# Mixers in plain units, output pairs that open with both first products, and sums between products

## The chip, the cores and the metric

The program runs on one core of one Trainium2 chip. The metric is the device time of one execution in microseconds (us). The engines are named as in the profile: PE does the matmuls, PEld their weight loads, DVE is the vector engine, ACT the scalar engine, POOL the general one, and SP issues the DMAs that bring the weights.

## The reference

Two blocks stand one behind the other on 512 positions of width 1024; all data are fp32. The first is a hybrid mixer (gated delta rule and retention) with a network behind it. The second has two layers, each a network, a mixer and a network, with a layer norm behind each of the three; this is its core:

```python
def swiglu_2(x, w1, w2):
    g, u = jnp.split(x @ w1, 2, axis=-1)
    return (jax.nn.silu(g) * u) @ w2
def hybrid_mixer_2(...):
    b_gate, c_gate, v, x_r, y_r, g_logits = jnp.split(x @ w_in, SPLITS, axis=-1)
    y_a = (b_gate * causal_depthwise_conv(c_gate * v, sc_w, 3)) @ w_out_conv
    xc = causal_depthwise_conv(x_r, rc_w, 4) + rc_b
    gates = jax.nn.sigmoid(per_head(xc, rg_w) + rg_b)      # 4 heads of 256, two gates each
    log_a = -8.0 * gates[1] * jax.nn.softplus(-a_param)
    a = jnp.exp(log_a); mult = jnp.sqrt(-jnp.expm1(2.0 * log_a))
    h = linear_recurrence(a, xc * gates[0] * mult)         # h_t = a_t h_(t-1) + b_t
    y_b = (h * jax.nn.gelu(y_r)) @ w_out_rnn
    g_a, g_b = jnp.split(jax.nn.sigmoid(g_logits + b_merge), 2, axis=-1)
    return (g_a * y_a + g_b * y_b) @ w_o
```

So the program has five networks (swiglu, inner width 2816) and, in its second block, two of these mixers.

## The kernel before

**Products.** Every fp32 product is made of three matmuls on rounded halves: an operand x is split into hi (a cast on ACT) and lo = x − hi (a subtraction on DVE), and hi·hi, hi·lo and lo·hi are added up in PSUM. The weights arrive in fp32 by DMA, 512 KB at a time (a raw tile `wraw`), and are split on the chip into `whi`, `wlo` (some tiles of the same kind lie in the big tile `xa` that also holds the activations, and carry its name).

**A plain unit** is one block of 128 output columns: one weight (`load_w`: load, cast L43, subtraction L44) and `mm3` (L70 to L72), 24 matmuls of 128x512. Plain units are ordered by the automatic scheduler.

**A seven-quad** (class `Quad`) makes 2 by 2 output blocks at once (two groups of 128 columns each way, halves of 256 positions), with seven products in place of eight, as Strassen's method does. A product is 24 matmuls of 128x256 (`prod`, L134; 18 where the inner part has three blocks, 12 with two). Before it, sums of weights are made on DVE (`sum`, L164), each is cast on ACT (`cast`, L167) and its rest taken on DVE (`rest`, L169), and the activations need sums too (`Left.sums`, L120 to L126, split at L80 and L81). Behind a product, `after` moves it out of or between the PSUM banks (ACT, L180 to L184) and then runs the steps that use it.

**run_quads** writes the order of a list of quads by hand: PE, ACT, DVE and SP run in the order in which the program was written. Its position s is one product; with the product at s it emits the copies behind product s−1, then the due sums, the cast for product s+2, the due steps, and the rest for s+2. The four weight blocks of a quad are loaded together, six positions ahead.

**A network** (`ffn`): two quads' worth of columns run in plain units (`PLAIN=2`; silu and `h`, L285 and L289), the others in seven-quads. The inner width is done in the groups (0,3), (3,3), (6,2), (8,3) of (first quad, how many). Behind each of the first three groups come two output quads, the *output pair*: they multiply this group's `h` (its halves are `hl`) with the second weight. The first of a pair waits for the group's `h` (`needs`). The activation sums that the seven-quads want (`e.sums`, and `H.sum4` for the columns of the plain units) are made while the plain units run.

**A mixer** (`mixer`): two of the four heads of the recurrent branch are projected in plain units, then come 12 seven-quads (`run(0,2)`, `run(2,5)`, `run(5,12)`) for the rest of the input weight, with the recurrent gates (`rgates`: two sigmoids per tile L542 and L543, exp L547, tanh L548, sqrt L551, the recurrence, and a split into `uh`, `ul`) and the plain products with `w_or` and `w_oc` between them. The residual `X` is parked in DRAM during the mixer, as its tile holds the mixer's sum `z`.

The sequence of the trace in us: first block to about 1003 (its network from 671), network 1003 to 1382, mixer 1382 to 1963 (its seven-quads with what lies between them 1433 to 1865), networks to 2293 and to 2675, mixer 2675 to 3260 (seven-quads 2726 to 3161), last network to 3607.

Of the kernel before, what the change touches and what calls it, by code (L numbers as in the profile page):

```python
# [434 lines left out]
def mixer(e, w, w_rg, w_oc, w_or, w_o, C, ln):  # L435

    nc=e.nc
    with ExitStack() as cm:
        mx=cm.enter_context(e.tc.tile_pool(name="mx",bufs=1,reuse_waits="tile"))
        uh=mx.tile([P,8,512],F32R,name="uh"); ul=mx.tile([P,8,512],F32R,name="ul"); U=Flat(uh,ul)  # L440
        xg=lambda nm: mx.tile([P,2,516],F32,tag="xg",name=nm,bufs=7)

        z=e.X
        for m in range(8): nc.gpsimd.dma_start(e.xs[:,m,:],e.X[:,m,:])
        R={}
        def rec(hd):

            u=Use(); R[hd]=u
            def c11(ps):
                u.xp=xg("xp"); nc.gpsimd.memset(u.xp[:,:,0:3],0.0)  # L450
                nc.scalar.copy(u.xp[:,:,3:259],pair(ps))
            def c12(ps,E):
                t=tmp(e); nc.vector.tensor_add(t,ps,E)
                u.gy=xg("gy"); nc.scalar.activation(u.gy[:,:,0:256],pair(t),AF.Gelu_apprx_tanh)
            def c22(ps,E):
                t=tmp(e); nc.vector.tensor_sub(t,E,ps)
                u.t=t
            def c21(ps):
# [944 lines left out]
```

## Time and profile before

| | us |
|---|---|
| median of 3 runs (3608.77 to 3612.39) | 3608.95 |
| profiled execution | 3608.84 |
| its span in the trace | 3607.0 |
| PE busy in it | 3296.6 |
| DVE busy | 2788.0 |
| ACT busy | 1830.2 |

The profiled execution took 1.84 us more than its span, the time that lies around it, and is 0.11 us below the median. A busy share is a mean over stages with different limits; the stage that an edit touches has to be read by itself.

### The profile page before, as it was taken

The numbers are of one execution on the slowest core, as the hardware profiler recorded it, in microseconds if no ns is written. First come the engines' busy times: TensorE is split into PE (matmuls) and PEld (weight loads), VectorE is DVE, ScalarE is ACT, GpSimd is POOL, SyncE is SP. The second block draws the span as 40 slices with busy tenths as digits, with TensorE's granted clock in tenths as the row PEclk, the third lists the DMA queues.
The fourth block names the chain that finished last, engine by engine and source line by source line (L and its number), as shares of the span: only waits on it lengthen the run. The fifth ranks groups of instructions, "written<-read, shape, count | busy, mean of one in ns | idle before, by whom it ended". The sixth has DMA issues, their size and how long they took to land.

```text
span 3607.0 us, 58745 instructions
## 1 busy us (share of the span) xinstructions
PE 3296.6 (91%) x23808; PEld 3094.0 (86%) x23808; DVE 2788.0 (77%) x4333; ACT 1830.2 (51%) x2794; POOL 193.6 (5%) x237
## 2 busy tenths in 40 slices
PE   7889889899989999789899999989998798998998
PEld 3768779799989999688889999989997698898998
DVE  5957878799768888856767888788888657667887
ACT  5544435455445555853434455445557733444554
POOL 3231210000000000000000000000000000000000
PEclk9989999999999999999999999999999999999999
DMA  5221225133322242122241323223331232422322
GB/s 200 71 65 45 77 65 173 32 101 99 111 72 93 86 138 82 59 97 74 88 153 48 101 85 117 81 82 99 97 120 51 73 96 86 139 86 66 103 94 65
DMA packets 106080, 330.74 MB, mean 92 GB/s; under 512 B 11984, under 2 KB 15696, under 8 KB 105808
## 3 DMA queue, kind: packets, MB, share of 16 engines
q1 hardware_dynamic: 102464, 316.04, 27.1%
q0 software_dynamic: 3200, 10.49, 0.8%
q8 instruction: 187, 3.06, 0.4%
q14 instruction: 85, 0.70, 0.1%
q10 hardware_dynamic: 144, 0.45, 0.0%
HBM read 320.64 MB, written 6.29 MB: 91 GB/s over the span
## 4 chain that ended last, share of the span: by engine, by line
PE 64%; DVE 19%; ACT 8%; issue 4%; DMA 3%; POOL 1%; ACTq 0%; SPq 0%; DVEq 0%; POOLq 0%
PE sd L134 19%; PE pj L134 15%; PE pj L70 5%; PE pj L71 5%; PE pj L72 5%; DVE wlo L169 3%; PE sd L70 3%; PE sd L72 3%; PE sd L71 3%; DVE wraw L164 3%; DVE xa L169 2%; ACT whi L167 2%; ACT xa L167 1%; DVE cv L933 1%; DVE hl L81 1%
## 5 line engine op out<-in xcount | busy, mean ns | idle before, releaser
L169 DVE TENSOR_TENSOR wlo<-wraw,whi 128x1024 fp32r<-128x1024 f32 (+2 forms) x398 | 444.8, 1118 | 113.1 <-ACT whi L167 111.5
L134 PE MATMUL sd<-xa,whi 128*128 128x256 f32 x3136 | 428.6, 290 | 50.2 <-ACT sd L182 29.3
L167 ACT CAST whi<-wraw 128x1024 fp32r<-128x1024 f32 (+2 forms) x398 | 380.7, 963 | 147.4 <-DVE wraw L164 64.4
L134 PEld LDWEIGHTS sd<-xa,whi 128*128 128x128 f32 x3136 | 404.0, 197 | 58.4 <-ACT sd L182 31.7
L134 PE MATMUL pj<-xa,whi 128*128 128x256 f32 x2096 | 294.2, 296 | 54.6 <-ACT sd L180 40.3
L134 PEld LDWEIGHTS pj<-xa,whi 128*128 128x128 f32 x2096 | 278.7, 204 | 61.5 <-ACT sd L180 44.0
L134 PE MATMUL pj<-xa 128*128 128x256 f32 x1824 | 241.0, 290 | 30.8 <-ACT xa L167 11.9
L169 DVE TENSOR_TENSOR xa<-wraw,xa 128x1024 fp32r<-128x1024 f32 (+2 forms) x196 | 216.8, 1106 | 61.1 <-ACT xa L167 53.6
L70 PE MATMUL pj<-xa 128*128 128x256 f32 (+1 forms) x760 | 258.7, 343 | 3.1 <-ACT xa L80 1.7
L134 PEld LDWEIGHTS pj<-xa 128*128 128x128 f32 x1824 | 231.7, 198 | 34.7 <-ACT xa L167 13.7
L72 PE MATMUL pj<-xa 128*128 128x256 f32 (+1 forms) x760 | 258.6, 341 | 0.2 <-DVE xa L44 0.2
L71 PE MATMUL pj<-xa 128*128 128x256 f32 (+1 forms) x760 | 257.4, 339 | 0.1
L134 PE MATMUL sd<-xa 128*128 128x256 f32 x1920 | 247.1, 285 | 9.8 <-ACT sd L182 7.9
L134 PEld LDWEIGHTS sd<-xa 128*128 128x128 f32 x1920 | 239.2, 194 | 10.6 <-ACT sd L182 8.3
L167 ACT CAST xa<-wraw 128x1024 fp32r<-128x1024 f32 (+2 forms) x196 | 186.8, 953 | 99.7 <-DVE wraw L164 45.6
L134 PE MATMUL sd<-xa,wlo 128*128 128x256 f32 x1568 | 225.7, 288 | 0.0
L164 DVE TENSOR_TENSOR wraw<-wraw 128x1024 f32<-128x1024 f32 (+2 forms) x198 | 221.6, 1119 | 0.0
L134 PEld LDWEIGHTS sd<-xa,wlo 128*128 128x128 f32 x1568 | 208.0, 197 | 0.1
L43 ACT CAST xa<-wraw 128x1024 fp32r<-128x1024 f32 (+1 forms) x126 | 127.5, 1013 | 158.2 <-PE pj L71 101.5
L70 PEld LDWEIGHTS pj<-xa 128*128 128x128 f32 x760 | 147.3, 195 | 15.5 <-ACT xa L80 1.9
L71 PEld LDWEIGHTS pj<-xa 128*128 128x128 f32 x760 | 147.7, 194 | 10.6 <-DVE xa L81 0.5
L44 DVE TENSOR_TENSOR xa<-wraw,xa 128x1024 fp32r<-128x1024 f32 (+1 forms) x116 | 137.8, 1189 | 23.9 <-ACT xa L43 23.1
(570 smaller groups left out, 7699.1 us busy)
## 6 DMA issues: line engine op xcount, KB each, us to landing
wraw<-in_f_dram SPq DMA_DIRECT2D x176, 512.0 KB, 3.6
wraw<-in_f_dram SPq DMA_DIRECT2D x96, 384.0 KB, 3.1
wraw<-in_ff_dram SPq DMA_DIRECT2D x44, 512.0 KB, 3.7
wraw<-in_win_dram SPq DMA_DIRECT2D x32, 512.0 KB, 3.6
wraw<-in_w_xy_dram SPq DMA_DIRECT2D x32, 512.0 KB, 3.5
wraw<-in_w_cv_dram SPq DMA_DIRECT2D x32, 512.0 KB, 3.5
raw<-in_ada_dram SPq DMA_DIRECT2D x48, 256.0 KB, 2.8
wraw<-in_ff_dram SPq DMA_DIRECT2D x24, 384.0 KB, 3.2
```

The source lines that it names most:

```text
L43: nc.scalar.copy(hi[:,:n],raw[:,:n])
L44: (nc.gpsimd if e.wi%e.gp==0 else nc.vector).tensor_sub(lo[:,:n],raw[:,:n],hi[:,:n].bitcast(F32))
L70: nc.tensor.matmul(o,lhsT=hi[:,c],rhs=ah,start=start and k==k0,stop=False)
L71: nc.tensor.matmul(o,lhsT=hi[:,c],rhs=al,start=False,stop=False)
L72: nc.tensor.matmul(o,lhsT=lo[:,c],rhs=ah,start=False,stop=stop and k==nk-1)
L81: e.nc.vector.tensor_sub(lo,src,hi.bitcast(F32))
L134: nc.tensor.matmul(ps[:,p*256:p*256+256],lhsT=w[:,j:j+128],rhs=A.t[:,c,k,l,:],start=first,stop=last,skip_group_check=True)
L164: n=s.n; e.nc.vector.tensor_add(o[:,:n],x[:,:n],y[:,:n])
L167: s.w[j]=hilo_tile(e); e.nc.scalar.copy(s.w[j][0][:,:s.n],s.raw(j)[:,:s.n])
L169: hi,lo=s.w[j]; n=s.n; e.nc.vector.tensor_sub(lo[:,:n],s.raw(j)[:,:n],hi[:,:n].bitcast(F32))
L933: nc.vector.scalar_tensor_tensor(a[:,o0:o0+n],ci[:,o0+i:o0+i+n],sc(i),a[:,o0:o0+n],op0=ALU.mult,op1=ALU.add)
```

## The change

Both mixers of the second block lose their seven-quads: all their products are plain units, in a new function `mixer_in`. Heads are projected one ahead of their gates (`rproj(hd)`, then `rgates(hd-1)`), the gate projections and the products with `w_or` alternate, then the conv branch runs column by column. `z` has a tile of its own, so the parking of `X` falls away (32 DMAs on POOL's queue), and one of the recurrence's multiplications moves from DVE to POOL. The activation sums are no longer made in the mixers. The ring of raw weight tiles has four in the mixers instead of five, and in the networks seven as before.

In run_quads an output pair starts with product 1 of both its quads, behind the seventh product of the group's last quad as before; the second quad's first product is copied out while the first quad's seventh runs. A quad's loads come in three parts, its fifth sum's tile is taken when the sum is made, and cast and rest for position s+2 both stand behind the steps. Of the activation sums of a network, the second part and those of `h` of the plain units go between products (`extra`, positions 0 to 2 and 4 and 5); the first block's network keeps the former in the plain part.

```diff
-    def load(s,e):
+    def load(s,e,t):
         n=s.n; q=s.q
-        s.r12=load_raw(e,q[2],n); s.r22=load_raw(e,q[3],n); s.t3=e.wps[0][0].tile([P,1024],F32,tag="t3",name="t3",bufs=1); s.r11=load_raw(e,q[0],n); s.r21=load_raw(e,q[1],n)
+        if t==0: s.r11=load_raw(e,q[0],n)
+        if t==5: s.r12=load_raw(e,q[2],n); s.r22=load_raw(e,q[3],n);
+        if t==6: s.r21=load_raw(e,q[1],n)
     def sum(s,e,t):
+        if t==3: s.t3=e.fp.tile([P,1024],F32,tag="t3",name="t3",bufs=1)
         o,x,y={1:(s.r12,s.r12,s.r11),2:(s.r11,s.r11,s.t3),3:(s.t3,s.r12,s.r22),4:(s.r21,s.r21,s.r11)}[t]
         n=s.n; e.nc.vector.tensor_add(o[:,:n],x[:,:n],y[:,:n])
-    def raw(s,j): return (None,s.r11,s.r21,s.r11,s.r12,s.t3,s.r22,s.r21)[j]
+    def raw(s,j): return getattr(s,(None,"r11","r21","r11","r12","t3","r22","r21")[j])
...
-def run_quads(e, quads):
+def run_quads(e, quads, extra):
     ET=mybir.EngineType
-    seq=[]; left=None
-    for q in quads:
+    seq=[]; left=None; done=set()
+    for i,q in enumerate(quads):
         if q.needs and left: seq.append((left,7)); left=None
-        seq.append((q,1))
+        if q not in done: seq.append((q,1))
+        if q.needs: seq.append((quads[i+1],1)); done.add(quads[i+1])
         if left: seq.append((left,7))
         seq+=[(q,j) for j in (2,3,4,5,6)]; left=q
     seq.append((left,7))
     pos={(id(q),j):s for s,(q,j) in enumerate(seq)}
-    at={}
+    at={}; free=-99
     for q in quads:
-        a=pos[id(q),1]
-        for s,t in ((a-6,0),(a-3,3),(a-1,1),(a,2),(pos[id(q),5],4)): at.setdefault(s,[]).append((q,t))
+        g=lambda j: pos[id(q),j]
+        for s,t in ((g(1)-6,0),(g(3)-9,5),(g(2)-8,6),(max(g(3)-6,free),3),(g(3)-4,1),(g(3)-3,2),(g(5),4)): at.setdefault(s,[]).append((q,t))
+        free=g(5)-1
     with e.tc.manual_schedule(engines={ET.PE,ET.Activation,ET.DVE,ET.SP}):
-        for s in range(-6,len(seq)+1):
+        for s in range(min(at),len(seq)+1):
             for q,t in at.get(s,[]):
-                if t==0: q.load(e)
+                if t in (0,5,6): q.load(e,t)
+            put=None; keep=None
+            if s>0: put=seq[s-1]
             if 0<=s<len(seq):
                 q,j=seq[s]
                 for d in q.needs:
                     if j==1: d.all(6)
                     if j==3: d.all(7)
-                early=s>0 and j==2 and seq[s-1]==(q,1)
-                if early: q.after(e,1)
+                if j==2 and put==(q,1): q.after(e,1); put=None
                 q.mm(e,j)
-            else: early=False
-            if s>0 and not early: seq[s-1][0].after(e,seq[s-1][1])
+                if j==7 and s+1<len(seq) and seq[s+1][1]==2: keep=seq[s+1][0]
+            if put and not (put[1]==1 and put[0] in done): put[0].after(e,put[1])
             for q,t in at.get(s,[]):
-                if t: q.sum(e,t)
-            nx=seq[s+2] if 0<=s+2<len(seq) else None
-            if nx: nx[0].cast(e,nx[1])
+                if t in (1,2,3,4): q.sum(e,t)
             for q in quads:
                 for j in (2,5,6,7):
-                    if s>0 and (q,j)!=seq[s-1]: q.step(j)
-            if nx: nx[0].rest(e,nx[1])
+                    if s>0 and (q,j)!=put: q.step(j)
+            if keep in done: keep.after(e,1)
+            for f in extra.get(s,[]): f()
+            nx=seq[s+2] if 0<=s+2<len(seq) else None
+            if nx: nx[0].cast(e,nx[1]); nx[0].rest(e,nx[1])
...
+def htile(e): return e.fp.tile([P,4,256],F32,tag="h",name="h",bufs=3)
...
-                if j%2: into_left(e,H,j//2,hs[j//2],0 if sl is H0 else 1,True)
-        e.sums(0)
+                if j%2: into_left(e,H,j//2,hs[j//2],0 if sl is H0 else 1,False)
+        for i in range(4): e.sums(0,i)
         for j in range(halves,2*PLAIN):
             unit(j,FULL)
-            for half in (0,1): into_left(e,H,j//2,hs[j//2],half,True)
-        e.sums(1)
+            for half in (0,1): into_left(e,H,j//2,hs[j//2],half,False)
+        if e.early:
+            for i in range(4): e.sums(1,i)
...
-                run_quads(e,Q)
+                x={} if e.early else {0:[lambda: e.sums(1,0)],1:[lambda: e.sums(1,1)],2:[lambda: e.sums(1,2),lambda: e.sums(1,3)]}
+                for i,q in enumerate(range(PLAIN)): x[4+i]=[lambda q=q: H.sums(e,q,hs[q][:,0:2,:],hs[q][:,2:4,:])]
+                run_quads(e,Q,x)
...
-        run=lambda a,b: run_quads(e,[Quad(e.XA,q,4,u) for q,u in Q[a:b]])
...
-        rec(0).plain(w["xy"][0],(H0,H1))
-        e.sums(0)
-        rec(1).plain(w["xy"][1],(FULL,)); e.sums(1)
-        seven_mode(e); rgates(0); rgates(1)
-        run(0,2); rgates(2); rgates(3); run(2,5)
-        for m in range(8): orproj(m)
-        run(5,12)
...
+def mixer_in(e, mx, w_in, w_rg, w_oc, w_or, w_o, C, ln):
+    nc=e.nc; plain_mode(e,0)
+    uh=mx.tile([P,8,512],F32R,name="uh"); ul=mx.tile([P,8,512],F32R,name="ul"); U=Flat(uh,ul)
+    B_,C_,V_,XR,YR,GA,GB=[8*i for i in range(7)]
+    n=512
+    xp={}; gy={}; xc={}
+    def rproj(hd):
...
+            ps=psum(e); mm3(e,ps,W[key],0,KD,e.XA,sl)
...
+                nc.scalar.copy(xp[t][:,3+sl.start:3+sl.stop],ps[:,:m])
+            else:
+                if t not in gy: gy[t]=mx.tile([P,512],F32,tag="gy",name="gy",bufs=3)
+                nc.scalar.activation(gy[t][:,sl],ps[:,:m],AF.Gelu_apprx_tanh)
...
+        wg=load_w(e,w_rg[hd])
+        xc2=Flat(uh[:,2*hd:2*hd+2,:],ul[:,2*hd:2*hd+2,:])
+        gp={}
+        for i,t in enumerate((2*hd,2*hd+1)):
+            pr=psum(e,"ps"); mm3(e,pr,wg,512+i*128,2,xc2,FULL,stride=256)
+            pi=psum(e,"ps"); mm3(e,pi,wg,i*128,2,xc2,FULL,stride=256)
+            gr=tmp(e); nc.scalar.activation(gr,pr,AF.Sigmoid,bias=C["rg_b"][:,8+t:9+t])
+            gi=tmp(e); nc.scalar.activation(gi,pi,AF.Sigmoid,bias=C["rg_b"][:,t:t+1])
+            gp[t]=(gr,gi)
...
+        for t in (2*hd,2*hd+1):
+            gr,gi=gp[t]
+            a=tmp(e); nc.scalar.activation(a,gr,AF.Exp,scale=C["nsp"][:,t:t+1])
+            th=gr; nc.scalar.activation(th,gr,AF.Tanh,scale=C["psp"][:,t:t+1])
+            a2=tmp(e); nc.gpsimd.tensor_mul(a2,a,a)
+            nc.vector.scalar_tensor_tensor(th,a2,1.0,th,op0=ALU.add,op1=ALU.mult)
...
+            nc.gpsimd.tensor_mul(gi,gi,xc[t])
...
+    rproj(0)
+    for hd in range(1,4): rproj(hd); rgates(hd-1)
+    gbproj(0); rgates(3)
+    for m in range(1,3): gbproj(m)
+    for m in range(8):
+        if 3<=m+2<8 and m>0: gbproj(m+2)
+        orproj(m)
...
+        wc=load_w(e,w_in[C_+m]); pc=psum(e); mm3(e,pc,wc,0,KD,e.XA,FULL)
+        ct=tmp(e); nc.scalar.copy(ct,pc)
...
+        wb=load_w(e,w_in[B_+m]); pb=psum(e); mm3(e,pb,wb,0,KD,e.XA,FULL)
+        nc.vector.tensor_mul(u,u,pb)
...
+    A=e.gab
+    for m in range(A-1): gproj(m)
+    for m in range(8):
+        if m+A-1<8: gproj(m+A-1)
+        cproj(m)
...
-        e.gp=1<<30; wp2=pool("wp2"); e.wps=[(wp2,2)]; e.rps.append((wp2,1)); e.more=2
+        e.gp=1<<30; wp2=pool("wp2"); e.wps=[(wp2,2)]; e.more=3; e.gab=GAB
```

Counted over the whole program, PE has 4032 matmuls of 128x256 fewer (24 quads of 168) and 2304 of 128x512 more (96 units of 24); DVE has 184 additions and subtractions of 128x1024 fewer, ACT 88 casts of that size and 120 smaller operations.

**PE, first output pair of the second network** (the stretch around 1073 to 1097 us of the trace). `hl` is the split h; `pj` and `sd` are PSUM banks. Before:

```order
L134 MATMUL sd0_5192<-xa_85 128x256 x24
L134 MATMUL pj_10581<-hl_9851,whi_10533 128x256 x12
L134 MATMUL pj_10581<-hl_9851,wlo_10534 128x256 x6
L134 MATMUL pj_10581<-hl_9851,whi_10566 128x256 x12
L134 MATMUL pj_10581<-hl_9851,wlo_10567 128x256 x6
L134 MATMUL sd1_5193<-hl_9851,xa_85 128x256 x18
L134 MATMUL pj_10661<-hl_9851,whi_10625 128x256 x12
L134 MATMUL pj_10661<-hl_9851,wlo_10626 128x256 x6
```

After:

```order
L134 MATMUL sd0_5189<-xa_85 128x256 x24
L134 MATMUL pj_10577<-hl_9848,whi_10532 128x256 x12
L134 MATMUL pj_10577<-hl_9848,wlo_10533 128x256 x6
L134 MATMUL pj_10602<-hl_9848,whi_10565 128x256 x12
L134 MATMUL pj_10602<-hl_9848,wlo_10566 128x256 x6
L134 MATMUL pj_10577<-hl_9848,xa_85 128x256 x18
L134 MATMUL sd1_5190<-hl_9848,whi_10629 128x256 x12
L134 MATMUL sd1_5190<-hl_9848,wlo_10630 128x256 x6
```

Before, the second product of the first output quad went into the bank of its first (`pj_10581` twice); now the second quad's first product, in a bank of its own (`pj_10602`), stands between them.

**ACT, the first recurrent gates of the second block's first mixer** (around 1508 us of the trace). `t` are gates, `vec`, `nsp` and `psp` constants. Before:

```order
L542 ACT_TABLE_LOAD
L542 ACTIVATE t<-ps,vec_9810 128x512
L543 ACTIVATE t<-ps,vec_9810 128x512
L542 ACTIVATE t<-ps,vec_9810 128x512
L167 CAST whi<-wraw 128x1024
L543 ACTIVATE t<-ps,vec_9810 128x512
L547 ACT_TABLE_LOAD
L547 ACTIVATE t<-t,nsp_9812 128x512
L548 ACTIVATE t<-t,psp_9813 128x512
L80 CAST uh<-xc 128x1024
L551 ACT_TABLE_LOAD
L551 ACTIVATE t<-t 128x512
```

After, a little into the same work:

```order
L482 ACT_TABLE_LOAD
L482 ACTIVATE gy<-sd_5189 128x512
L497 ACT_TABLE_LOAD
L497 ACTIVATE t<-ps,vec_9807 128x512
L498 ACTIVATE t<-ps,vec_9807 128x512
L43 CAST xa<-wraw 128x1024
L502 ACT_TABLE_LOAD
L502 ACTIVATE t<-t,nsp_9809 128x512
L503 ACTIVATE t<-t,psp_9810 128x512
L479 COPY xp<-sd_5191 128x512
L506 ACT_TABLE_LOAD
L506 ACTIVATE t<-t 128x512
```

The gelu of the next head's projection (L482) now stands between the gates of this one, with a table load of its own; from the first gate to the last split of the branch there are 27 table loads, 49 activations of 128x512, 17 casts of 128x1024, 13 casts and 4 copies of 128x512 on ACT, beside 402 matmuls of 128x512 on PE.

**DVE, behind the plain part of the second network** (from 1050 us of the trace). `h` of the last plain unit, its split, then the sums. Before:

```order
L289 SCALAR_TENSOR_TENSOR h<-t,sd_5193 128x2x256
L164 TENSOR_TENSOR wraw<-wraw 128x1024
L81 TENSOR_TENSOR hl<-h,hl 128x2x256
L81 TENSOR_TENSOR hl<-h,hl 128x256
L120 TENSOR_TENSOR s<-h 128x256
L169 TENSOR_TENSOR wlo<-wraw,whi 128x1024
L121 TENSOR_TENSOR s<-s,h 128x256
L164 TENSOR_TENSOR wraw<-wraw,t_10337 128x1024
L123 TENSOR_TENSOR s<-s,h 128x256
L169 TENSOR_TENSOR wlo<-wraw,whi 128x1024
L81 TENSOR_TENSOR hl<-s,hl 128x4x256
```

After:

```order
L298 SCALAR_TENSOR_TENSOR h<-t,sd_5190 128x2x256
L167 TENSOR_TENSOR wraw<-wraw,t_10300 128x1024
L81 TENSOR_TENSOR hl<-h,hl 128x2x256
L81 TENSOR_TENSOR hl<-h,hl 128x256
L172 TENSOR_TENSOR wlo<-wraw,whi 128x1024
L122 TENSOR_TENSOR s<-X 128x256
L125 TENSOR_TENSOR s<-X 128x256
L126 TENSOR_TENSOR s<-s 128x256
L81 TENSOR_TENSOR xa<-s,xa 128x2x256
L172 TENSOR_TENSOR wlo<-wraw,whi 128x1024
```

The sums of the input (L122 to L126) now stand between the rests of the first quad's weights (L172), and the sums of `h` come later; from this `h` to the last split of the first quad's `h` DVE has 10 operations of 128x1024, 4 of 128x768, 10 of 128x512 and 21 of 128x256.

## Rows read from the trace of the kernel before

**Rows 1.** The page: span, and busy time of each engine with its instructions.

```profile
span 3607.0 us, 58745 instructions
PE 3296.6 (91%) x23808; PEld 3094.0 (86%) x23808; DVE 2788.0 (77%) x4333; ACT 1830.2 (51%) x2794; POOL 193.6 (5%) x237
```

**Rows 2.** Busy time by stage; columns are in the first row.

```profile
core 0: us, PE busy (x) PEld busy (x) DVE busy (x) ACT busy (x) POOL busy (x), PEclk, DMA share, GB/s
1003.00:1382.00 379.00, 360.07 (x2823) 352.21 (x2822) 308.20 (x411) 192.40 (x279) 0.00 (x0) 0.97 0.29 95
1433.00:1537.00 104.00, 75.63 (x464) 66.28 (x463) 83.17 (x101) 82.95 (x103) 9.10 (x14) 0.93 0.17 56
1433.00:1865.00 432.00, 375.26 (x2505) 347.66 (x2504) 300.33 (x330) 228.00 (x293) 15.39 (x28) 0.96 0.28 92
2293.00:2675.00 382.00, 362.50 (x2837) 354.25 (x2836) 314.94 (x426) 195.56 (x286) 0.00 (x0) 0.97 0.29 92
2726.00:3161.00 435.00, 378.20 (x2503) 350.51 (x2503) 300.24 (x329) 227.83 (x292) 15.45 (x28) 0.95 0.28 91
```

**Rows 3.** The same view of three short stretches, for the pace of matmuls.

```profile
1610.00:1650.00 40.00, 40.00 (x178) 33.14 (x177) 16.71 (x17) 7.38 (x7) 0.10 (x1) 1.00 0.25 81
1125.00:1175.00 50.00, 50.00 (x419) 50.00 (x418) 42.32 (x48) 27.79 (x37) 0.00 (x0) 1.00 0.27 85
1686.90:1690.30 3.40, 3.40 (x18) 3.40 (x17) 3.37 (x4) 0.84 (x2) 0.00 (x0) 0.50 0.02 5
```

**Rows 4.** PE's waits from 1433 to 1865: waited for, total us, times, longest.

```profile
PE sd L134 <- ACT sd L182: 20.3, 7, 5.2
PE pj L134 <- ACT sd L180: 12.0, 7, 4.0
...
PE ps L70 <- ACT t L543: 4.5, 2, 2.3
PE ps L70 <- ACT uh L80: 3.8, 1, 3.8
```

**Rows 5.** ACT's operations by form, 1433 to 1537: busy, mean ns, idle before.

```profile
L167 ACT CAST whi<-wraw 128x1024 fp32r<-128x1024 f32 x9 | 9.3, 1035 | 0.5 <-PE ps L71 0.5
L547 ACT ACT_TABLE_LOAD x7 | 9.0, 1283 | 0.1
...
L542 ACT ACTIVATE t<-ps,vec 128x512 f32<-128x512 f32 x8 | 5.5, 686 | 1.7 <-PE ps L72 1.7
...
L80 ACT CAST uh<-t 128x512 fp32r<-128x512 f32 x6 | 3.7, 620 | 3.6 <-DVE t L557 3.6
```

**Rows 6.** ACT's timeline from 1507.2: start, duration, operation, idle before.

```profile
1507.39 1.05 ACT L167 CAST xa<-wraw 128x1024 fp32r<-128x1024 f32 x1 [0.39 <-DMA wraw<-in_w_gb_dram]
1508.46 1.28 ACT L542 ACT_TABLE_LOAD   x1
1509.75 0.69 ACT L542 ACTIVATE t<-ps,vec 128x512 f32<-128x512 f32 x1
```

**Rows 7.** PE's timeline, output pairs of the second network, rows with idle before.

```profile
1090.68 1.70 PE L134 MATMUL pj<-hl,whi 128*128 128x256 f32 x12 [1.48 <-ACT sd L180]
...
1095.00 1.22 PE L134 MATMUL sd<-hl,xa 128*128 128x256 f32 x8 [0.82 <-DVE hl L81]
...
1185.57 1.65 PE L134 MATMUL pj<-hl,whi 128*128 128x256 f32 x6 [1.49 <-ACT sd L180]
...
1259.23 1.21 PE L134 MATMUL pj<-hl,whi 128*128 128x256 f32 x8 [1.25 <-ACT sd L180]
...
1262.01 0.39 PE L134 MATMUL sd<-hl,xa 128*128 128x256 f32 x1 [0.61 <-ACT hl L80]
1263.27 0.93 PE L134 MATMUL sd<-hl,xa 128*128 128x256 f32 x4 [0.87 <-DVE hl L81]
```

**Rows 8.** All engines from that `h` to the first quad's last `hl`.

```profile
1050.41:1087.81 37.40, 28.35 (x184) 26.75 (x183) 27.38 (x42) 14.71 (x21) 0.00 (x0) 0.82 0.14 43
```

**Rows 9.** DVE's operations by form in the second network.

```profile
L169 DVE TENSOR_TENSOR wlo<-wraw,whi 128x1024 fp32r<-128x1024 f32 x37 | 45.2, 1222 | 6.2 <-ACT whi L167 6.1
...
L169 DVE TENSOR_TENSOR wlo<-wraw,whi 128x768 fp32r<-128x768 f32 x15 | 14.3, 954 | 2.6 <-ACT whi L167 2.5
...
L81 DVE TENSOR_TENSOR hl<-h,hl 128x512 fp32r<-128x512 f32 x14 | 9.7, 689 | 8.2 <-ACT hl L80 8.2
...
L379 DVE TENSOR_TENSOR lnQ<-lnQ,t 128x256 f32<-128x256 f32 x11 | 4.3, 419 | 0.1
```

**Rows 10.** A weight's load: issues, KB each, median us from issue to landing.

```profile
wraw<-in_w_xy_dram SPq DMA_DIRECT2D x32, 512.0 KB, 3.5
```

More of the change, by code (lines that the diff above doesn't have):

```diff
@@ L234 @@
 class Use: pass
-def htile(e): return e.fp.tile([P,4,256],F32,tag="h",name="h",bufs=2)
+def htile(e): return e.fp.tile([P,4,256],F32,tag="h",name="h",bufs=3)
 def into_left(e, H, i, h, half, sums):
@@ L265, in gated @@
     return u
+GAB=4
 GROUPS=((0,3),(3,3),(6,2),(8,3))
@@ L427, in finish, with proj_units @@
             if s.out is None: s.to_left(sl,i,X[:,2*i:2*i+2,sl])
-        if sl is H1: e.sums=lambda part: [e.XA.sums(e,i,X[:,2*i:2*i+2,H0],X[:,2*i:2*i+2,H1],part) for i in range(4)]
+        if sl is H1: e.sums=lambda part,i: e.XA.sums(e,i,X[:,2*i:2*i+2,H0],X[:,2*i:2*i+2,H1],part)
+def proj_units(units, first):
+    out=[]
+    if first:
+        for s in (H0,H1):
+            for u in units[:first]: out.append((u,s))
+    for u in units[first:]: out.append((u,FULL))
+    return out
 def zsplit(e, m, x):
@@ L433, in zsplit, with mixer @@
     split(e,v[:,:,0,:],v[:,:,1,:],pair(x))
[L435 to L437 removed]
+def mixer(e, w_in, w_rg, w_oc, w_or, w_o, C, ln):
     with ExitStack() as cm:
[L439 to L458, printed above, removed]
[L459 to L580 removed]
@@ L626, in second @@
         ffn(e,D["f1"][l][0],D["f2"][l][0],acc,0.5,mk(0))
-        mixer(e,{k:D["w_"+k][l] for k in QCOLS},D["rg"][l],D["woc"][l],D["wor"][l],D["wo"][l],C,mk(1,r=ALPHA))
+        mixer(e,D["win2"][l],D["rg"][l],D["woc"][l],D["wor"][l],D["wo"][l],C,mk(1,r=ALPHA))
         o=None
@@ L670, in ffn2_quads @@
     return res
-QCOLS={"xy":[(24+t,25+t,32+t,33+t) for t in (0,2,4,6)],"gb":[(48+t,49+t,50+t,51+t) for t in (0,4)],
-    "b":[(t,t+1,t+2,t+3) for t in (0,4)],"cv":[(8+t,9+t,16+t,17+t) for t in (0,2,4,6)],"ga":[(40+t,41+t,42+t,43+t) for t in (0,4)]}
 def vcol(v):
@@ L681, in host2 @@
     D["f2"]=np.stack([np.stack([pack_ffn2(i["ffn_w2_2"][l,j]) for j in range(2)]) for l in range(2)])
-    for k,v in QCOLS.items(): D["w_"+k]=np.stack([pack_some(i["w_in_2"][l],v,2 if k=="xy" else 0) for l in range(2)])
+    D["win2"]=np.stack([pack_cols(i["w_in_2"][l]) for l in range(2)])
     D["rg"]=np.stack([np.ascontiguousarray(i["rg_w_2"][l].reshape(2,4,2,128,256).transpose(1,3,0,2,4).reshape(4,128,1024)) for l in range(2)])
@@ L688, in dram2 @@
 def dram2(D):
-    R={n:D[n] for n in ("vec2","rg","woc","wor","wo","f1",*("w_"+k for k in QCOLS))}
+    R={n:D[n] for n in ("vec2","rg","woc","wor","wo","f1","win2")}
     R["f2"]=[[ffn2_quads(D["f2"][l,j]) for j in range(2)] for l in range(2)]
@@ L1266, in again, with sums @@
             nc.vector.tensor_add(t,A[:,o:o+2,i,0,:].bitcast(F32),A[:,o:o+2,i,1,:].bitcast(F32)); return t
-        def sums(part):
-            for i in range(4):
-                if s.b is None: e.XA.sums(e,i,X[:,2*i:2*i+2,H0],X[:,2*i:2*i+2,H1],part)
-                else: e.XA.sums(e,i,again(i,0),again(i,2),part)
-        if sl is H1: e.sums=sums
+        def sums(part,i):
+            if s.b is None: e.XA.sums(e,i,X[:,2*i:2*i+2,H0],X[:,2*i:2*i+2,H1],part)
+            else: e.XA.sums(e,i,again(i,0),again(i,2),part)
+        if sl is H1: e.sums=sums; e.early=s.b is not None
 def ada_piece(e,D,at,part,k,tag,raw):
@@ L1372, in build @@
         e.fixed=e.places[:2]
-        dp=ctx.enter_context(tc.tile_pool(name="dp",bufs=1,space=bass.MemoryType.DRAM))
-        e.xs=dp.tile([P,8,512],F32,name="xs")
         with ExitStack() as ca:
```

169 lines of the change are left out of this document (58 added, 111 removed).

## The prediction

> **What bounds the kernel now.** I read the page first: PE is busy 3296.6 of 3607.0 us [rows 1], so what PE does and what it waits for is nearly the whole time, but the mean hides that the stages differ. Busy time by stage shows it [rows 2]: a network keeps PE at 360 of 379 us, the mixers' seven-quad stretches only at 375 of 432 and 378 of 435. A busy PE is not yet a PE at full pace, so the next thing is the pace of the two kinds of matmul, where nothing interrupts them [rows 3]: 176 of 128x512 in 40 us (178 rows, two of them at the edges) is 0.2275 us each, 417 of 128x256 in 50 us is 0.120 us each. Where the granted clock reads 0.50, that is the lower of the two levels (1.2 instead of 2.4 GHz), a 128x256 takes about 0.21 us [rows 3]. Stretches of 3.4 us at this level follow stalls of PE, and one of them holds some 15 matmuls that lose 0.09 each, so about 1.4 us on top of the stall.
>
> By these paces a mixer's stretch needs 12 x 168 = 2016 matmuls of 128x256 (241.9 us) and 480 of 128x512 (8 units with w_or, 8 with w_oc, four heads' gates; 109.2 us), together 351 us; the 2505 rows of the first agree [rows 2]. So 432 - 351 = **81 us** are lost there and 435 - 351 = **84 us** in the second mixer. Where they go says the list of PE's waits [rows 4]: 20.3 and 12.0 us are waits of seven-product matmuls for ACT's copies between banks (L182, L180), and some 8 us waits of plain ones for gate sigmoids and for the split `uh`. The rest is the lower clock behind such stalls.
>
> A network has (2688 x 0.120) + (84 x 0.2275) = 342 us of matmuls in its 379 us [rows 2]: 37 us lost. They lie in few places: behind its plain part, from the last plain `h` (1050.41) to the last split of the first quad's `h`, PE is busy 28.35 of 37.40 us at a mean clock of 0.82 [rows 8], and each of the three output pairs opens with a stall of 1.25 to 1.49 us for the copy of the bank in which its first product has just ended, with smaller waits for `hl` behind it [rows 7].
>
> **The mixers, part by part.** Twelve quads a mixer fall away, -2016 x 0.120 = -241.9 us, and 1152 matmuls of 128x512 come, +262.1: **+20 us of PE work a mixer**, certain and paid in full. What this buys is that the seven-product waits have nowhere left to be. In the conv branch and the products with w_or and w_oc a plain unit is 24 x 0.2275 = 5.46 us of PE; DVE has one rest of 1.22 us [rows 9] and a few operations of 0.7, ACT one cast of 1.04 [rows 5] and an activation of 0.69. The stretch 1610 to 1650 is that kind of work before, and PE is busy in all of its 40 us at full clock [rows 3]. I take the loss there as nothing; what hides the split work is the 5.46 us, and without that cover 1.04 + 1.22 a unit would come in.
>
> The other end is the recurrent front. From the first gate to the last split ACT has 27 table loads of 1.283, 49 activations of about 0.69, 17 casts of 1.05 and 17 casts and copies of about 0.61: 34.6 + 33.8 + 17.9 + 10.4 = **97 us** [rows 5], beside 402 x 0.2275 = **91.5 us** of PE. So ACT, not PE, sets the end there. How well ACT can be filled is not in the trace for this order. Below, nothing idle: 97 - 91.5 = 5.5 us lost. Above, the idle share of the nearest stretch before, 1433 to 1537, where the first gates lie: ACT busy 82.95 of 104 us [rows 2], so 97/0.80 = 121, 30 us lost. Its waits there are short ones for DVE and PE between gate steps (3.6 us for the recurrence, 1.7 for products [rows 5]); in the new order the next head's projection stands between the gates and feeds ACT. I take 90 %, 97/0.9 = 108: **16 us lost a mixer**. Mixers: -(81 - 20 - 16) = -45 and -(84 - 20 - 16) = -48, **-93 us**.
>
> A table load stands here as its own row: cast at 1507.39 of 1.05, load at 1508.46 of 1.28, activation at 1509.75 [rows 6], so each begins where the one before ended and a switch costs 1.28 us. The Trainium skill ("ScalarE: Activation LUTs", What ACT_TABLE_LOAD costs) gives 1283 ns for the load, as here, and a further drain of about 1380 ns for each switch. By it the 27 loads would cost 27 x 1.38 = 37 us more a mixer. These rows show no such gap, and the sum goes without it.
>
> The residual need no longer be parked: 32 DMAs leave POOL's queue, and POOL, busy 15.39 of 432 us [rows 2], takes 8 multiplications a mixer off DVE; neither is on the path, nothing. The sums of activations that DVE made for the mixers' quads, and 88 casts and 184 rests, leave engines that wait for PE or are waited for only in the front; that is in the figures above. One raw tile fewer in the mixers: a weight lands 3.5 us after its issue [rows 10], one is used up each 5.46 us, and four tiles hold 22 us of work, so nothing; the price if it fails is the last rival.
>
> **The networks, part by part.** Output pair: the stall of 1.48 us for L180 and then 0.82 for `hl` [rows 7] are covered by the second quad's first product, 18 x 0.120 = 2.2 us, which needs only what the first one needed. First pair **2.2**. Second pair: the stall of 1.49 [rows 7], all of it under 18 matmuls, **1.5**. Third pair (12 matmuls, 1.44 us): 1.25 goes, of the 0.61 and 0.87 for `hl` about two thirds go, as those have 1.44 us longer, **2.2**. With a stall gone the lower clock behind one of them goes too in some place, **1.4**. A network gains 2.2 + 1.5 + 2.2 + 1.4 = 7.3, and all five do: **-37 us** (the copy that the second quad owes later runs under the first's seventh, 18 x 0.120 = 2.2 us against a copy of 0.58).
>
> Sums between products and loads in parts: in the stretch of [rows 8] DVE is busy 27.38 of 37.40 us before. After, the same stretch (h to the last `hl`) holds 10 x 1.22 + 4 x 0.95 + 10 x 0.69 + 21 x 0.42 = 31.7 us of DVE [rows 9], since the weight rests of the second output quad now lie in it. With some 4 us of waits for ACT it ends where it did, 36 us: **nothing**. Best end: DVE never waits, 37.4 - 31.7 = 5.7 us a network. Worst: the casts that now stand behind the steps, one a product, come later by a step of 0.6 to 0.7, and half of the pairs' gain goes, -3.7 a network. So the networks lie between 3.6 and 13 us each, 18 to 65 in all.
>
> **Sum.** 3608.8 - 93 - 37 = **3479 us**; the 3608.84 of the profiled execution is its span of 3607.0 and 1.8 around it, and is the median of the runs within 0.1. The front's ends (5.5 and 30 us a mixer, -21 and +28) and the networks' (-28 and +19) give 3430 to 3526 at the very ends, 3450 to 3505 for the case itself.
>
> **Rivals.**
> 1. *PE bounds the front too.* ACT's rows need not fit between the first gate and the last split: casts go ahead while heads 0 and 1 are projected, and PE has the gate projections and the w_or products to run beside the last recurrences. Then the 16 us a mixer are not lost: 3479 - 32 = **3447**. For it: PE has plain work at hand; against it: ACT is in order, and `h` of the last head is needed by every product with w_or.
> 2. *ACT costs the front 30 us or more.* With its old idle share, 3479 + 2 x (30 - 16) = **3507** (0.09). Where each change of function also held ACT up by as much again as its load, 27 x 1.28 = 35 us a mixer, it would be 3479 + 70 = **3549** (0.04). For both: sigmoids, gelu, exp and sqrt alternate, so loads can't be shared; against: the extra idle before each load is not in [rows 6]. The skill's page above gives this second case with its own figure: 37 us a mixer, 3553.
> 3. *Slower: weights come late.* All 168 weights of the two mixers are loaded one by one through four raw tiles. If one is had only every 5.46 + d us, the mixers lose 168 d; the whole gain of 130 is gone at d = 0.78, that is one weight in 6.24 us instead of 5.46. Against it: 3.5 us from issue to landing [rows 10] and DMA share 0.25 in a stretch of such units at full pace [rows 3]. At d = 1, 3479 + 168 = **3647**.
> 4. *It does nothing*: the +20 of PE and the front take all of the mixers' 81 and 84, and the networks' copies only move. That takes a front loss of 61 us a mixer, ACT 153 us long with 97 of work: about **3609**.
>
> **How the numbers follow.** Forecast 0.68, rival 1 0.14, rival 2 0.13, rival 3 0.03, rival 4 0.02. The predicted time is the forecast's, 3479. Range for 8 in 10: from 3425 (rival 1 with some of the networks' best end) to 3525 (the front's bad end with the networks' worst), leaving out the far part of rival 2 and rivals 3 and 4. 0.2 % is 7.2 us, about what a measurement of this kernel can tell from no change: faster means under 3601.7. Forecast and rivals 1 and 2 are faster (0.95), of rival 4 half (0.01); same 0.01, slower 0.03.
>
> **What would show it.** Right: in the mixers no wait of a product for L180 or L182; after the front PE idles almost nothing; PE's front waits are for sigmoids or `uh`, and it lasts 105 to 110 us against 91.5 of work; in the networks the output pairs open without the 1.25 to 1.49 us stalls; the first quad's `hl` still comes 36 us after the last plain `h`. Wrong: a front whose PE waits sum below 5 or above 30 us, waits of casts for `wraw` DMAs in the conv branch, or new stalls at the quad's first products behind later casts.

## The result, and the profile after

The changed kernel takes 3473.78 us (median of 4 runs, 3472.77 to 3474.55) against 3608.86 before: a ratio of 0.9626, 95% interval 0.9609 to 0.9643. The forecast was 3479 in 3425 to 3525. The total hides two errors of opposite sign, as the stages tell.

The page after, span and busy time of each engine, which answers to [rows 1]:

```profile
span 3471.3 us, 54695 instructions
...
PE 3272.6 (94%) x22056; PEld 2997.8 (86%) x22056; DVE 2538.6 (73%) x4061; ACT 1701.5 (49%) x2600; POOL 200.1 (6%) x237
```

Busy time by stage after, with the columns of [rows 2]: the second network; the first mixer from its first gate products to the end of the products with w_oc; its front, up to the last wait of PE; what follows; the second mixer.

```profile
995.40:1369.40 374.00, 356.19 (x2826) 349.38 (x2825) 308.52 (x411) 192.85 (x280) 0.14 (x2) 0.99 0.30 96
1419.50:1796.50 377.00, 373.10 (x1633) 306.68 (x1632) 183.51 (x210) 166.08 (x197) 23.26 (x35) 1.00 0.30 95
1421.00:1523.00 102.00, 98.10 (x421) 79.34 (x420) 66.88 (x77) 87.80 (x106) 22.57 (x28) 0.98 0.27 83
1523.00:1796.00 273.00, 273.00 (x1204) 225.69 (x1205) 116.08 (x134) 76.80 (x91) 0.69 (x7) 1.00 0.32 100
2651.80:3029.00 377.20, 373.24 (x1634) 306.89 (x1632) 183.53 (x210) 166.25 (x197) 23.37 (x35) 1.00 0.30 95
```

The mixers' 432 and 435 us [rows 2] are 377 each: 55 and 58 us gained where 45 and 48 were forecast. Of 1632 matmuls of 128x512 at 0.2275, 371.3 us, PE loses 5.7 us. Behind the front it is busy in all 273 us. The waits of seven-product matmuls [rows 4] are gone; these are all that PE has in the first mixer (waited for, total us, times, longest):

```profile
PE ps L70 <- ACT t L497: 2.1, 2, 1.7
PE ps L70 <- ACT uh L80: 1.3, 1, 1.3
PE ps L71 <- DVE ul L81: 0.3, 1, 0.3
PE pj L71 <- DVE ul L81: 0.2, 1, 0.2
```

The second network gained 5 us (379 to 374), not 7.3. PE's timeline of its first output pair after (start, duration, operation, and in brackets the idle time before it):

```profile
1073.76 1.22 PE L134 MATMUL pj<-hl,whi 128*128 128x256 f32 x8 [1.70 <-ACT whi L170]
1077.14 0.38 PE L134 MATMUL pj<-hl,whi 128*128 128x256 f32 x1 [2.16 <-ACT hl L80]
1078.82 1.01 PE L134 MATMUL pj<-hl,whi 128*128 128x256 f32 x3 [1.30 <-DVE hl L81]
...
1098.21 2.06 PE L134 MATMUL pj<-hl,xa 128*128 128x256 f32 x15 [1.67 <-ACT sd L183]
```

The opening's own stall, 1.48 us in [rows 7], is gone, but PE now waits before the pair's products for weights and `hl`, and 1.67 us at its end for L183, the copy of the second quad's first product. ACT's timeline at the two places, and DVE's at the second, say why:

```profile
1071.93 1.04 ACT L80 CAST hl<-s 128x1024 fp32r<-128x1024 f32 x1 [3.06 <-DVE s L123]
1072.88 1.56 ACT L170 CAST whi<-wraw 128x768 fp32r<-128x768 f32 x2
1076.46 0.62 ACT L80 CAST hl<-h 128x512 fp32r<-128x512 f32 x1 [2.02 <-DVE h L260]
...
1097.59 0.57 ACT L183 COPY sd<-pj 128x512 f32<-128x512 f32 x1 [2.28 <-DVE X L607]
```

```profile
1096.82 0.68 DVE L607 TENSOR_TENSOR X<-X,sd 128x512 f32<-128x512 f32 x1
```

ACT stood 3.06 us for a sum of `h` (one of those moved between products) with the weight casts for the pair behind it. The copy at 1097.59 did not wait for ACT: by the profile it waited for L607, an update of `X` on DVE, which ended at 1097.50. That update reads the bank of the first quad's fifth product, and as three `sd` banks are used in turn, this is the bank that the copy writes.

### The profile page after: what moved, and what is told of

It is laid out like the page before. It is cut to its first block, busy times and chain, and to the rows that moved or that the text cites. A ratio compares the mean times of both kernels' runs of the same rounds, so it can differ in the third digit from the quotient of the medians.

```text
span 3471.3 us, 54695 instructions
## 1 busy us (share of the span) xinstructions
PE 3272.6 (94%) x22056; PEld 2997.8 (86%) x22056; DVE 2538.6 (73%) x4061; ACT 1701.5 (49%) x2600; POOL 200.1 (6%) x237
## 4 chain that ended last, share of the span: by engine, by line
PE 70%; DVE 16%; ACT 6%; issue 5%; POOL 1%; DMA 1%; ACTq 0%; SPq 0%; DVEq 0%; POOLq 0%
PE sd L134 15%; PE pj L134 12%; PE pj L70 7%; PE pj L71 6%; PE pj L72 6%; PE sd L70 6%; PE sd L71 6%; PE sd L72 6%; DVE wraw L167 2%; DVE wlo L172 1%; DVE cv L913 1%; ACT whi L170 1%; DVE xa L172 1%; DVE X L607 1%; DVE xa L44 1%
## 5 line engine op out<-in xcount | busy, mean ns | idle before, releaser
L172 DVE TENSOR_TENSOR wlo<-wraw,whi 128x1024 fp32r<-128x1024 f32 (+2 forms) x310 | 333.5, 1076 | 57.8 <-ACT whi L170 54.0
L44 DVE TENSOR_TENSOR xa<-wraw,xa 128x1024 fp32r<-128x1024 f32 (+1 forms) x188 | 229.3, 1221 | 180.3 <-ACT xa L43 179.7
L70 PE MATMUL pj<-xa 128*128 128x512 f32 (+1 forms) x960 | 336.0, 352 | 3.3 <-ACT xa L80 1.7
L72 PE MATMUL pj<-xa 128*128 128x512 f32 (+1 forms) x960 | 336.3, 351 | 0.2 <-DVE xa L44 0.2
L71 PE MATMUL pj<-xa 128*128 128x512 f32 (+1 forms) x960 | 335.3, 350 | 0.1
L170 ACT CAST whi<-wraw 128x1024 fp32r<-128x1024 f32 (+2 forms) x310 | 286.4, 930 | 48.9 <-DVE wraw L167 24.4
L134 PE MATMUL sd<-xa,whi 128*128 128x256 f32 x2080 | 271.5, 283 | 1.9 <-ACT sd L185 1.9
L134 PEld LDWEIGHTS sd<-xa,whi 128*128 128x128 f32 x2080 | 259.6, 192 | 2.3 <-ACT sd L185 2.3
L70 PE MATMUL sd<-xa 128*128 128x512 f32 (+1 forms) x688 | 233.8, 342 | 2.7 <-ACT xa L80 1.7
L71 PE MATMUL sd<-xa 128*128 128x512 f32 (+1 forms) x688 | 234.8, 342 | 0.0
L72 PE MATMUL sd<-xa 128*128 128x512 f32 (+1 forms) x688 | 234.0, 341 | 0.0
L134 PE MATMUL pj<-xa,whi 128*128 128x256 f32 x1360 | 183.7, 289 | 20.4 <-ACT sd L183 20.3
L172 DVE TENSOR_TENSOR xa<-wraw,xa 128x1024 fp32r<-128x1024 f32 (+2 forms) x140 | 152.4, 1088 | 57.5 <-ACT xa L170 19.2
L134 PEld LDWEIGHTS pj<-xa,whi 128*128 128x128 f32 x1360 | 174.4, 198 | 22.7 <-ACT sd L183 22.7
L134 PE MATMUL sd<-xa 128*128 128x256 f32 x1200 | 155.6, 287 | 8.7 <-ACT sd L187 8.7
L134 PEld LDWEIGHTS sd<-xa 128*128 128x128 f32 x1200 | 150.5, 196 | 9.8 <-ACT sd L187 9.8
```

The lines of the kernel that those rows point to most:

```text
L44: (nc.gpsimd if e.wi%e.gp==0 else nc.vector).tensor_sub(lo[:,:n],raw[:,:n],hi[:,:n].bitcast(F32))
L70: nc.tensor.matmul(o,lhsT=hi[:,c],rhs=ah,start=start and k==k0,stop=False)
L71: nc.tensor.matmul(o,lhsT=hi[:,c],rhs=al,start=False,stop=False)
L72: nc.tensor.matmul(o,lhsT=lo[:,c],rhs=ah,start=False,stop=stop and k==nk-1)
L134: nc.tensor.matmul(ps[:,p*256:p*256+256],lhsT=w[:,j:j+128],rhs=A.t[:,c,k,l,:],start=first,stop=last,skip_group_check=True)
L170: s.w[j]=hilo_tile(e); e.nc.scalar.copy(s.w[j][0][:,:s.n],s.raw(j)[:,:s.n])
```

## The experiments

Twelve kernels ran, each time being the median of four or five executions. The intervals are those of the ratio to the kernel before.

**The mixers alone.** The mixers of the change with `run_quads`, loads and sums of before.

> The plain mixers of the change with the networks of before (their order of products, loads and sums; only the tile of the fifth weight sum lies in the network's pool so that it fits). By the terms of the prediction the networks give 37 us, so this should be 3474 + 37 = 3511 us. By the stages of the trace after, the mixers gave 55 and 57 us and everything else 23, so it should be 3609 - 112 = 3497 us.

3482.53 us, ratio 0.9656 (0.9643 to 0.967), faster than either expectation. With the plain mixers alone 126 of the 135 us are there; all of the networks' edits together are worth 9 us. PE's timelines say where, in us: up to the first seven-product matmul (L134); from the first to the last of them in each network, all five together; from a network's last to the next network's first where a mixer lies between, both together.

| | first block | five networks' seven-quads | two mixers and what lies around them |
|---|---|---|---|
| before | 673 | 1462 | 1242 |
| the mixers alone | 667 | 1457 | 1125 |
| the change | 667 | 1444 | 1130 |

So the mixers themselves gave 117, and some 11 lie in the first block and in the networks, whose order is that of before. The networks' edits gave 13 us in the seven-quads, and 5 were lost again around the mixers.

**The bank.** One line in run_quads (`openers` holds the first quads of the pairs, `done` the second ones):

```diff
+            if put and put[1]==5 and put[0] in done|openers: put[0].all(5)
```

> The change, but in the output pairs both additions that use the fifth product's bank stand together, right behind it. Theory of the bank: the copy of the second quad's first product waits for the second of these additions, which still reads the bank that the copy wants; then the waits of 1.8, 1.0 and 2.1 us that close the three first quads of a pair go, up to 4.9 us a network, 25 us in all: 3450 us, or 3460 if half returns elsewhere. Rival: the copy is late because ACT and DVE are late as a whole (a cast that waits for its load); then no change, 3474 us within 4.

3439.16 us, 0.9538 (0.9524 to 0.9551): 35 us, more than the 25 of the stalls alone. ACT's timeline at the same copy, now right behind its cast:

```profile
1087.11 0.84 ACT L170 CAST xa<-wraw 128x768 fp32r<-128x768 f32 x1 [1.59 <-DMA wraw<-in_f_dram]
1087.85 0.58 ACT L183 COPY sd<-pj 128x512 f32<-128x512 f32 x1
```

The cast still waits for its load, so that was not what held the copy. The bank was.

**Sums of h in the plain part again.**

```diff
-                if j%2: into_left(e,H,j//2,hs[j//2],0 if sl is H0 else 1,False)
+                if j%2: into_left(e,H,j//2,hs[j//2],0 if sl is H0 else 1,True)
...
-                for i,q in enumerate(range(PLAIN)): x[4+i]=[...H.sums(...)]
```

> The change, but the sums of h of the plain units are made in the plain part again; the input's sums stay between products. If DVE's work in the first quad sets when the first pair may start, its 5.8 us (two times 4 x 0.42 and 1.23) leave that stretch and each network gains 3 to 5 us: 3449 to 3459 us. If the stretch is set by waits between DVE and ACT for the quad's own copies, or the plain part gets as much longer, it stays at 3474 us within 5.

3451.96 us, 0.9573 (0.9559 to 0.9587): 22 us, as the first theory said.

**More table loads.**

```diff
+            dm=mx.tile([P,1],F32,...); nc.scalar.activation(dm,gr[:,0:1],AF.Gelu_apprx_tanh)
```

> The change with one more gelu of one column in every tile of the recurrent gates, whose result nothing uses: 16 more activations and about 30 more table loads on ACT in the two fronts. If ACT sets the end of the fronts and a load costs its 1.28 us: 30 x 1.28 + 16 x 0.2 = 42 us, less some 5 of slack a mixer, 3505 to 3516 us. If each load also holds ACT up by a drain of 1.38 us as the Trainium skill has it (ScalarE: Activation LUTs, What ACT_TABLE_LOAD costs), an estimate of 41 us more: 3546 to 3557 us. If PE bounds the fronts and ACT has room (it is busy 87.8 of 102 us in the first front), at most the part beyond 14 us a mixer shows: 3474 to 3488 us.

3517.25 us, 0.9753 (0.974 to 0.9767): 43 us more. The trace has 15 loads more in each mixer, and the first mixer's stretch grew from 377 to 398 us:

```profile
1424.00:1822.00 398.00, 377.98 (x1634) 309.00 (x1633) 182.25 (x210) 187.26 (x221) 23.54 (x35) 0.97 0.28 90
```

15 x 1.283 + 8 x 0.203 (the small activations) is 20.9 us, and 398 - 377 is 21. Each load cost its own duration in full, so ACT does set the front's end. The Trainium skill ("ScalarE: Activation LUTs", What ACT_TABLE_LOAD costs) adds a drain of about 1380 ns to every switch; an estimate by it is 42 us a mixer for these loads, and this run does not bear it out.

**No opening.**

```diff
-        if q.needs: seq.append((quads[i+1],1)); done.add(quads[i+1])
```

> The change, but an output pair no longer opens with both first products: the second quad's first product comes behind the first's fifth and sixth as before. If the opening is worth what the prediction gave it (2.2 + 1.5 + 2.2 us a network without the lower clock, 29 us in all), 3474 + 29 = 3503 us. If the wait for the bank takes it back (1.8, 1.0 and 2.1 us a network, as the trace after shows), the opening is worth about 5 us in all: 3474 to 3484 us.

3470.86 us, 0.962 (0.9607 to 0.9633): the change without its opening is 3 us faster, within what can be told from none. As the change stands, the wait for the bank takes back all that the opening gives. With the bank free it gives 32 us (3470.86 against the 3439.16 above).

**The input's sums ahead.**

```diff
-        if e.early:
+        if True:
...
-                x={} if e.early else {...}
+                x={} if True else {...}
```

(with the sums of h left between products)

> The change, but the second part of the input's sums is made ahead of the seven-quads in all networks, those of h stay between products. If the copy behind the first product is late because ACT, in order, stands at the split of such a sum (3.5 us of idle before it in the second network), each of four networks gains about 3 us: 3462 us. If the sums' DVE work is in the way wherever it stands, since the plain part has no room on DVE for it at its end, 3474 us within 6, or up to 15 more where the first product has to wait for them.

3448.88 us, 0.956 (0.9547 to 0.9574): 25 us, twice what the first theory gave. In the second network the wait for the first quad's copy (under ACT's split of a sum) shrank from 2.67 us after the change to 0.66 here:

```profile
1050.11 2.24 PE L134 MATMUL pj<-xa,whi 128*128 128x256 f32 x12 [2.67 <-ACT sd L183]
...
1048.47 1.21 PE L134 MATMUL pj<-xa,whi 128*128 128x256 f32 x8 [0.66 <-ACT sd L183]
```

That is 2 of the some 6 us that each of the four networks gained; the rest was not followed.

**Together.**

> The change with the two additions together behind the fifth product, and the sums of h in the plain part. The two alone gave 35 and 22 us. If they act in different places (closing of the pairs, and the first quad up to its h) they add up: 3474 - 57 = 3417 us. If both free DVE in the same stretch and one is enough, 3435 us.

3413.77 us, 0.9463 (0.945 to 0.9476): 60 us, a little over the sum of the two (56).

> As the run with both, and the second part of the input's sums ahead of the quads too, so that no sum is left between products. If DVE is the limit from the plain part's end on, the place of these sums matters little: within 6 us of the run with both. If ACT's order is the limit, 10 to 15 us faster than it; if the first seven-product matmuls now wait for the sums, slower by as much.

3414.57 us, 0.9465 (0.9452 to 0.9478): no difference. One set of sums out of the first quad is enough.

**The opening with its obstacle gone.** All sums ahead, without the opening.

> As the run with all sums ahead of the quads, but the pairs don't open with both first products (and so without the bank that made a copy wait, and without the two additions together). Beside it this sizes the opening with its obstacle gone: by the prediction's 2.2 + 1.5 + 2.2 us a network it is worth 29 us, and this takes 3415 + 29 = 3444 us. If the opening never was worth much, because the pairs' time is set by DVE's splits of h and not by the copy, 3415 to 3425 us.

3439.52 us, 0.9533 (0.952 to 0.9547): 25 us slower than with the opening. So the opening is worth 25 of the 29 us that the prediction gave it, once the copy may run.

**Fewer table loads.** On top of the run with both:

```diff
         for t in (2*hd,2*hd+1):
...
+            a2=z[:,t,:]; nc.gpsimd.tensor_mul(a2,a,a)
...
+        for t in (2*hd,2*hd+1):
+            th,gi=gp[t]
             nc.scalar.activation(th,th,AF.Sqrt)
```

> As the run named both, with the recurrent gates of a head in two passes: exp and tanh of both its tiles, then both square roots (the square of a stands in z, which is free by then). It has some 9 table loads fewer a mixer, 11.5 us of ACT. If ACT sets the end of the front, all that PE loses there (some 6 us a mixer) comes back: 3414 - 12 = 3402 us. If PE bounds the front, or the two passes make the gates later than the loads made them earlier, 3410 to 3418 us.

3408.07 us, 0.9448 (0.9434 to 0.9462), the fastest here. Its first mixer by stage:

```profile
1399.70:1771.70 372.00, 370.65 (x1633) 305.90 (x1632) 182.32 (x210) 153.55 (x188) 23.23 (x35) 1.00 0.30 96
```

372.0 for 371.3 us of matmuls: next to nothing is lost any more. The stretch is 5 us shorter than after the change (377 to 372) though 9 loads, 11.5 us, are gone; beyond 5 us PE is the bound. Against the run with both, the one that it was built on, the two stretches give 3.5 and 5.1 us by PE's timelines. The total fell by 5.7; runs of one kernel lie as far apart as that (3410.36 to 3417.86 for the run with both).

**The order of the casts.** Two runs have no opening and all sums ahead of the quads: the mixers alone (3482.53), and all sums ahead without the opening (3439.52). They differ by 43 us. The order of the casts was undone in the latter, and done alone in the former:

```diff
+            nx=seq[s+2] if 0<=s+2<len(seq) else None
+            if nx: nx[0].cast(e,nx[1])
             for q in quads:
...
-            if nx: nx[0].cast(e,nx[1]); nx[0].rest(e,nx[1])
+            if nx: nx[0].rest(e,nx[1])
```

> As the run with the sums ahead and no opening, but the cast for the product two positions on stands ahead of the steps again and only its rest behind them, as in the kernel before. That run (3440 us) and the one with the mixers alone (3483 us) differ by 43 us, though in the networks they differ in little but this order and the loads in parts. If the order of the casts is the cause, 3475 to 3483 us; if it is the loads, 3440 us within 5.

3460.87 us, 0.9594 (0.9581 to 0.9607): 21 us slower, between the two expectations. With the cast ahead of the steps, ACT casts a weight before a split of `h`. ACT's timeline behind the copy in the first pair, in this run and in the one with the casts behind the steps:

```profile
1075.20 0.57 ACT L183 COPY sd<-pj 128x512 f32<-128x512 f32 x1 [0.92 <-PE pj L134]
1075.68 0.84 ACT L170 CAST whi<-wraw 128x768 fp32r<-128x768 f32 x1
1076.42 0.41 ACT L80 CAST hl<-h 128x256 fp32r<-128x256 f32 x1
...
1072.03 0.57 ACT L183 COPY sd<-pj 128x512 f32<-128x512 f32 x1 [0.93 <-PE pj L134]
1072.52 0.41 ACT L80 CAST hl<-h 128x256 fp32r<-128x256 f32 x1
1072.82 0.83 ACT L170 CAST whi<-wraw 128x768 fp32r<-128x768 f32 x1
```

That this order is what the 21 us come from is shown by the edit; how they come, only in part. In the two traces the five networks' seven-quads are 16 us longer with the old order, but PE idles only 5 us longer in them; for the other 11 it is busy, with the same matmuls at a slower pace.

> As the run with the mixers alone (networks of before), and the cast moved behind the steps, next to its rest: this one part of the networks' change alone. If the order of the casts is what gives 43 us, 3440 to 3447 us; if it is the loads in parts, 3483 us within 5.

3482.29 us, 0.9652 (0.9638 to 0.9665): nothing. So the cast behind the steps gives 21 us, but only with the loads and sum times of the change, and these give 22 (3483 to 3461). A row of before shows what held there, ACT's timeline at the first pair's copy:

```profile
1089.31 0.83 ACT L167 CAST xa<-wraw 128x768 fp32r<-128x768 f32 x1 [1.72 <-DVE wraw L164]
1090.05 0.58 ACT L180 COPY sd<-pj 128x512 f32<-128x512 f32 x1
```

The cast waits for a sum of weights, and the copy stands behind it. The change makes that sum one position earlier where no seventh product lies between (`g(3)-3` is then the position ahead of the first product). In the run with old casts the cast starts at 1073.45, and the copy, at 1075.20 above, has only PE to wait for:

```profile
1073.45 0.83 ACT L170 CAST xa<-wraw 128x768 fp32r<-128x768 f32 x1
```

That the earlier sum is the whole of the 22 us, and not the loads in parts or the third tile for `h` that came with them, was not tried by itself.

## Why the prediction was right, and where its steps were not

That the total came within 5 us is luck: the run with the mixers alone gives 126 us where 93 were forecast for them, and the networks' edits 9 where 37 were.

- **Mixers, -93: mechanism right, undersized.** By the stages it was -55 and -58, -113. The +20 of PE work and the zero behind the front were right (273.0 of 273.0 busy). The term that was off is the front's loss of 16 us a mixer: PE lost 5.7 in the whole stretch. It was ACT that set the end, as assumed (more loads: every one paid). From the first gate's table load to the last split, with just the 110 operations on ACT that the prediction counts, the front lasts about what it said, 108.94 us for 108 (108.95 in the second mixer; the 102 above end at PE's last wait):

```profile
1420.44:1529.38 108.94, 105.04 (x450) 84.72 (x449) 72.25 (x82) 91.81 (x110) 22.66 (x29) 0.98 0.27 83
```

But the 108 came of two errors that cancel. 97 us was a sum of durations that overlap; the 110 operations keep ACT busy for 91.81 us, and that fills 84% of the front, not 90%. ACT's timeline after:

```profile
1480.14 0.69 ACT L497 ACTIVATE t<-ps,vec 128x512 f32<-128x512 f32 x1
1480.73 0.68 ACT L498 ACTIVATE t<-ps,vec 128x512 f32<-128x512 f32 x1
1481.30 1.05 ACT L43 CAST whi<-wraw 128x1024 fp32r<-128x1024 f32 x1
```

Each starts about 0.1 us before the one ahead has ended. What made the loss small is PE's side: it ran 450 matmuls in the front, not 402. That is 102.4 us of work, and 6.6 us are lost. The prediction had named PE waits below 5 us in the front as a sign that it was wrong, and they sum to 3.9: the sign was good for this term.
- **Networks, -37: too much, and for other reasons.** The mixers alone say 9 us, the trace 5 in the second network. Three steps failed.

The opening (5.9 a network) was right in itself, but "a copy of 0.58 under 2.2 us" looked at the copy's duration and not at the bank that it writes: what it needed was an update on DVE.

*Sums between products: nothing* was wrong. Beside the kernel before it looks right: the last `hl` came 35.9 us after the plain `h` (1042.90 to 1078.76), as forecast. DVE was busy 29.58 us in it and not 31.7, as its rows overlap too. But without these sums the rest of the change would have brought `hl` forward. DVE's rows of the plain `h` and of the last split of the first quad's `h`, first in the run without the opening, then in the one without the opening and with all sums ahead:

```profile
1042.08 0.68 DVE L297 SCALAR_TENSOR_TENSOR h<-t,sd 128x512 f32<-128x512 f32 x1
1077.94 0.68 DVE L81 TENSOR_TENSOR hl<-h,hl 128x512 fp32r<-128x512 f32 x1
...
1037.37 0.68 DVE L298 SCALAR_TENSOR_TENSOR h<-t,sd 128x512 f32<-128x512 f32 x1
1069.91 0.69 DVE L81 TENSOR_TENSOR hl<-h,hl 128x512 fp32r<-128x512 f32 x1
```

To the end of the split it is 36.5 us with the sums between products and 33.2 with the sums ahead. Over the whole program the sums cost 31 us without the opening (3470.86 to 3439.52).

The cast behind the steps, costed as a loss at worst, gives 21 us, the loads and sum times 22. The prediction had named new stalls at a quad's first products behind later casts as a sign of being wrong, and the 1.70 us for `whi` above are such a stall; but there the cast is late behind the split of a sum. In the order in which they were undone, from the mixers alone to the change: -22 - 21 + 31 + 3 = -9.

- **Rivals.** Rival 1 (PE bounds the front) is refuted as a bound by the run with more loads, though its time for the mixers was nearer, and its argument that PE has other work at hand beside the front is what the 450 matmuls show. Rival 2's extra stall per load is not there. Late weights (rival 3) are not seen: PE is busy without a gap behind the front. Rival 4's loss of 61 us in the front is not there either.
- **Two readings** in the prediction are off, and nothing in its sum hangs on them. PE idles 56.7 of the 432 us [rows 2], so of the 81 lost the lower clock had 24, and not all that is left beside the waits it lists. And of the "184 rests" 96 are sums of weights.
- **The first block** starts its seven-quads at 673.1 us before and at 666.6 after, by PE's timeline, with the plain part's code ahead of it hardly touched. In the twelve other runs it is 666.9 to 671.0. Some 2 to 6 us of the gain lie there; their cause is open. There is one trace of the kernel before, whose runs range from 3599.91 to 3613.24, so this may be no effect of the change.

## What to carry to other kernels

A copy that moves a product out of the way is as early as the bank that it goes to is free: look for the last reader of its destination, not only at its length. Where engines run in a written order, work that is free on one engine can stand in front of another's: price a moved sum by what waits behind the operation that waits for it, and against the rest of the change, not against the kernel before. A loss beside a long chain is the chain's length less the work that the other engine finds to do: both have to be counted. And a total that fits can be two wrong terms; reading the stages and moving one part at a time showed 66 us here that the change had left (3473.78 to 3408.07).

## What the runs showed of the hardware

Rows of ACT overlap by about 0.1 us, so their means add up to more than the engine's time (97 against 91.81 for the same 110 operations). A table load costs its 1.283 us and no more: 15 more of them, with eight small activations, made a stretch that ACT bounds 21 us longer. The granted clock is 1.00 in the plain mixers, where the seven-quads with their stalls had 0.96 and 0.95.
